# Convolutions accumulated in the projection's PSUM bank, scores moved into the transposes' bank, and a fourth bank for the SSD projections

## The chip, the core and the metric

One core of a Trainium2 chip runs the whole program. The metric is the device time of one execution in microseconds. TensorE (PE), VectorE (DVE), ScalarE (ACT) and GpSimd (POOL) compute, SyncE (SP) issues the loads and stores. Matmuls write to PSUM, which has eight banks of 128 partitions by 512 float32 values; VectorE and ScalarE read and write PSUM, GpSimd doesn't.

## What is computed

One step of a recurrent decoder layer for 2048 prompt tokens and 64 sample tokens (8 sequences of 8), with 1024 model dimensions. The tokens are normalised, projected with `w_in`, and go through three branches; the branches are gated, joined, projected with `w_out`, added to the input and normalised again. Cut to what matters here:

```python
proj = rmsnorm(x, norm_g) @ w_in
z, xbc, dt_raw, lru_x, lru_gate, s5_u, s5_gate = split(proj)
# SSD branch
xbc = silu(conv4(xbc, ssd_conv_w) + ssd_conv_b)        # depthwise, 4 taps
xs, bm, cm = split(xbc)
# per chunk of 128 tokens, per group of 4 heads:
scores = cm @ bm.T                                      # "scores"
y_diag = (scores * decay * dt) @ xs
y_off  = (cm @ h) * exp(acum);  h = chunk_decay * h + (bm * to_end * dt).T @ xs
y_ssd = rmsnorm((y_diag + y_off + d * xs) * silu(z))
# RG-LRU branch
xr = conv4(lru_x, lru_conv_w) + lru_conv_b
y_lru = linear_scan(f(xr @ lru_wa), g(xr @ lru_wx, xr)) * silu(lru_gate)
# S5 branch ...
out = x + concat(y_ssd, y_lru, y_s5) @ w_out
```

## The kernel before

The tokens stand in five segments: four of 512 prompt tokens (s = 0 to 3) and one of 64 sample tokens (s = 4). A projection (`in_proj`, L236 to L251) takes a block of 128 columns of `w_in` and one segment: 24 matmuls (eight parts of the contraction, each high by high, low by high and high by low in float16) add up in one PSUM bank, the tile `ps_mm`. The banks of the pool `pmm` (three of them) are taken in turn. The pool `ptp` has two banks (`ps_tp`, transposes), and the pool `pss` has three single ones with the tags "g", "y" and "s".

The program goes through these stages: the normalisation and the S5 branch, then the RG-LRU branch (`emit_lru`, about 430 to 705 us of the trace), then the SSD branch (`ssd_group` for four groups of heads, about 705 to 1380 us), then the output projection.

A channel block of the SSD branch (`channels` in `ssd_group`) runs so: ScalarE evicts the projection to `raw` in SBUF (`conv_raw`, L398), which ends the use of its bank. ScalarE writes the first tap and the bias to the tile `x` (L411), VectorE adds the other three taps in place (L413, three instructions), ScalarE takes the tanh of it into `th` (L699), and VectorE makes silu of the two (L700). The RG-LRU branch has the same convolution, without silu, into `xr`.

A chunk (`ssd_chunk`, 16 prompt chunks for each group) runs so: three transposes into `ps_tp` (L603, L604), of which VectorE makes `xdt` (L608) and ScalarE copies `bs` (L610); the scores matmul into the bank "g" (`ps_g`, L578), which ScalarE copies to `gm` (L587) and GpSimd masks (L588); VectorE multiplies the decays `e` with it (L589). Then come eight matmuls into the bank "y" (`ps_y`, L626 with `e`, L629 with the state `hst` and the decayed `ce`, which GpSimd makes at L596 out of a loaded row), the state product into the bank "s" (`ps_s`, L631), the state's update (L635 on GpSimd, L636 on VectorE) and the addition of `ps_y` to `x` (L640). The next chunk's `ps_y` waits for L640. The sample segment has one chunk for each group. The groups 2 and 3 also project their gates (`gated`, L710); those of the groups 0 and 1 were projected earlier and are loaded.

No order is written out by hand. A scheduler of the language orders each engine's instructions when the program is built, by a cost model of its own, within what dependences, tile buffers and banks allow; on the chip each engine then runs its list in order. Buffers that count here: `th` has two (the squares `sq` of the gated rows use them too), `ce` two, `raw` three, `x` five.

Of the kernel before, what the change touches and what calls it, by code (L numbers as in the profile page):

```python
# [43 lines left out]
def hymba_step_kernel(  # L44
# [16 lines left out]
    def bank(pool, tag, name):  # L61
        return pool.tile([128, 512], F32, name=name, tag=tag)
# [22 lines left out]
    def col(nm, i, src=cols):  # L85
        c = COL[nm] + i
        return src[:, c:c + 1]
# [145 lines left out]

    XH, XL = {}, {}

    def in_proj(w, s):  # L236

        n = SEGS[s][1]
        blocks = list(WB.values())
        for i, b in enumerate(blocks):  # L240
            if b.done is None and blocks[i - 6].left:
                b.age += 1
                if b.age > AGE:
                    b.finish()
            b.left = b.left or (b.w is w and s == 3)
        ps = bank(pmm, "mm", "ps_mm")
        for k in range(KD):
            P.matmul(ps[:, :n], lhsT=w[:, 0, k, :], rhs=XH[s][:, k, :], start=(k == 0), stop=False)  # L248
            P.matmul(ps[:, :n], lhsT=w[:, 0, k, :], rhs=XL[s][:, k, :], start=False, stop=False)  # L249
            P.matmul(ps[:, :n], lhsT=w[:, 1, k, :], rhs=XH[s][:, k, :], start=False, stop=(k == KD - 1))  # L250
        return ps[:, :n]  # L251
# [148 lines left out]
        G.tensor_copy(tl.halo, raw[:, SG:SG + 3])  # L400
        return raw

    def conv(out, raw, s, w, b):
        if s == 4:
            o = out.rearrange("p (b e) -> p b e", e=8)
            rv = raw.rearrange("p (b e) -> p b e", e=11)
            tap = [rv[:, :, j:j + 8] for j in range(4)]
        else:
            o = out
            tap = [raw[:, j:j + SG] for j in range(4)]  # L410
        A.activation(out=o, in_=tap[0], func=AF.Identity, scale=w[0], bias=b)  # L411
        for j in range(1, 4):
            V.scalar_tensor_tensor(o, tap[j], w[j], o, op0=ALU.mult, op1=ALU.add)  # L413

    def gate(ps, un2, s):

        n = SEGS[s][1]
        th = seg_tile("th", "th", s, st)
        pz = seg_tile("pz", "pz", s, st)
        A.activation(out=th, in_=ps, func=AF.Tanh, scale=un2)  # L420
        V.scalar_tensor_tensor(pz, th, 1.0, ps, op0=ALU.add, op1=ALU.mult)  # L421
        return pz
# [149 lines left out]

    sqacc = {}

    def scores(sp, g, BT, CT, q0, n, bcq, c):

        gp = bank(pss, "g", "ps_g")
        P.matmul(gp[:n, :n], lhsT=BT[:, q0:q0 + n], rhs=CT[:, q0:q0 + n], start=True, stop=True)  # L578
        e = sp.tile([128, 4, 128], F32, name="e", tag="e")
        gm = sp.tile([128, 128], F32, name="gm", tag="gm")[:n, :n]  # L580
        for h in range(4):
            A.activation(out=e[:n, h, :n], in_=bcq[:n, h, :n], func=AF.Relu, scale=-1.0, bias=acum[:n, c, 4 * g + h:4 * g + h + 1])  # L582
        A.activation(out=e[:n, :, :n], in_=e[:n, :, :n], func=AF.Exp, scale=-1.0)
        if c == 16:
            V.tensor_tensor(gm, gp[:n, :n], tri_s, op=ALU.mult)
        else:
            A.copy(gm, gp[:n, :n])  # L587
            G.affine_select(out=gm, in_=gm, pattern=[[1, n]], compare_op=ALU.is_ge, fill=0.0, base=0, channel_multiplier=-1)  # L588
        V.tensor_tensor(e[:n, :, :n], e[:n, :, :n], gm.unsqueeze(1).to_broadcast([n, 4, n]), op=ALU.mult)  # L589
        return e  # L590
# [8 lines left out]
    def transposed(sp, xs, BT, q0, n, g, c):  # L599

        tp = bank(ptp, "tp", "ps_tp")
        for j in range(2):
            P.transpose(tp[:n, j * 128:(j + 1) * 128], xs[j][:, q0:q0 + n], id32)  # L603
        P.transpose(tp[:n, 256:384], BT[:, q0:q0 + n], id32)  # L604
        xdt = sp.tile([128, 4, 64], F32, name="xdt", tag="xdt")
        xw = sp.tile([128, 4, 64], F32, name="xw", tag="xw")
        bs = sp.tile([128, 128], F32, name="bs", tag="bs")
        V.tensor_tensor(xdt[:n], tp[:n, 0:256].rearrange("p (h e) -> p h e", h=4),  # L608
                        dt_all[:n, c, 4 * g:4 * g + 4].unsqueeze(2).to_broadcast([n, 4, 64]), op=ALU.mult)
        A.copy(bs[:n], tp[:n, 256:384])  # L610
        G.tensor_tensor(xw[:n], xdt[:n], te[:n, c, 4 * g:4 * g + 4].unsqueeze(2).to_broadcast([n, 4, 64]), op=ALU.mult)
        return xdt, xw, bs

    def ssd_chunk(sp, g, xs, BT, CT, c, H):
        q0 = (c * 128) % SG
        bcq = sp.tile([128, 4, 128], F32, name="bcq", tag="bcq")
        S.dma_start(out=bcq, in_=aT[c, 4 * g:4 * g + 4, :].unsqueeze(0).to_broadcast([128, 4, 128]))
        xdt, xw, bs = transposed(sp, xs, BT, q0, 128, g, c)
        m = scores(sp, g, BT, CT, q0, 128, bcq, c)
        yp = bank(pss, "y", "ps_y")  # L620
        if c:
            ce = c_decayed(sp, CT, q0, 128, eT[c, 4 * g:4 * g + 4, :])
        o = [yp[64 * (h % 2):64 * (h % 2) + 64, (h // 2) * 128:(h // 2) * 128 + 128] for h in range(4)]
        for j in range(2):
            for h in (2 * j, 2 * j + 1):
                P.matmul(o[h], lhsT=xdt[:, h, :], rhs=m[:, h, :], start=True, stop=(c == 0))  # L626
            if c:
                for h in (2 * j, 2 * j + 1):
                    P.matmul(o[h], lhsT=H[:, h, :], rhs=ce[:, h, :], start=False, stop=True)  # L629
        ps = bank(pss, "s", "ps_s")  # L630
        P.matmul(ps[:, 0:256], lhsT=bs, rhs=xw.rearrange("p h e -> p (h e)"), start=True, stop=True)  # L631
        hn = sp.tile([128, 4, 64], F32, name="hst", tag="hst")
        spv = ps[:, 0:256].rearrange("p (h e) -> p h e", h=4)
        if c:
            G.tensor_tensor(hn, H, dec[:, c, 4 * g:4 * g + 4].unsqueeze(2).to_broadcast([128, 4, 64]), op=ALU.mult)  # L635
            V.tensor_tensor(hn, hn, spv, op=ALU.add)  # L636
        else:
            V.tensor_copy(hn, spv)
        for j in range(2):
            V.scalar_tensor_tensor(xs[j][:, q0:q0 + 128], xs[j][:, q0:q0 + 128], dpair[:, 2 * g + j:2 * g + j + 1],  # L640
                                   yp[:, j * 128:(j + 1) * 128], op0=ALU.mult, op1=ALU.add)
        return hn

    def ssd_sample(sp, g, xs, BT, CT):
# [4 lines left out]
        for q in range(2):  # L649
            hb = sp.tile([128, 4, 4, 64], F32, name="hb", tag="hb", bufs=2)  # L650
            S.dma_start(out=hb, in_=ssd_st[g, :, 4 * q:4 * q + 4])
            hbs.append(hb)
        xdt, xw, bs = transposed(sp, xs, BT, 0, n, g, 16)
        m = scores(sp, g, BT, CT, 0, n, bcq, 16)
        ce = c_decayed(sp, CT, 0, n, eTs[4 * g:4 * g + 4, :])
        for j in range(2):
            yp = bank(pss, "y", "ps_y")
# [9 lines left out]
        for q in range(2):  # L667
# [11 lines left out]
                V.tensor_tensor(hv, hv, ps, op=ALU.add)  # L679
            S.dma_start(out=o_ssd_s[g, :, 4 * q:4 * q + 4], in_=hb)  # L680

    def ssd_group(sx, sp, g, done):
        blks = [2 * g, 2 * g + 1, 8 + g, 12 + g]
        ws = [WB[c0] for c0 in SB(g)]
# [4 lines left out]
        def channels(i, s):  # L689

            w, un, _ = ws[i]
            b = blks[i]
            raw = conv_raw(in_proj(w, s), un, s, tls[i], stS[:, b, :])
            if s == 3:
                w_ahead()
            x = seg_tile("xxbc"[i] + str(i % 2), "x", s, sx if i < 2 else sp, SG, 5 if i < 2 else 2)
            conv(x, raw, s, [col("sconv_w", 16 * j + b, hcols) for j in range(4)], col("sconv_b", b, hcols))
            th = seg_tile("th", "th", s, st)
            A.activation(out=th, in_=x, func=AF.Tanh)  # L699
            V.scalar_tensor_tensor(x, th, 1.0, x, op0=ALU.add, op1=ALU.mult)  # L700
            return x

        def gated(j, s, y):
            k = 2 * g + j
            s0, n = SEGS[s]
            if k < ZE:
                pz = seg_tile("pz", "pz", s, st)
                S.dma_start(out=pz, in_=zb[k, :, s0:s0 + n])
            else:
                pz = gate(in_proj(WB[k][0], s), WB[k][2], s)  # L710
                if s == 3:
                    w_ahead()
            V.tensor_tensor(y, y, pz, op=ALU.mult)
            if g == 0 and j == 0:
                sqacc[s] = sx.tile([128, SEGS[s][1]], F32, name="sqacc", tag=f"sqacc{s}", bufs=1)
                rows[j].add(s, y, sqacc[s])
            else:
                sq = seg_tile("th", "sq", s, st)
                rows[j].add(s, y, sq)
                G.tensor_tensor(sqacc[s], sqacc[s], sq, op=ALU.add)  # L720
# [42 lines left out]
    def emit_lru(lp, blocks):  # L763
        for b in blocks:
# [8 lines left out]
            for grp in LRU_ORD:  # L773
                L = []
                for s in grp:
# [3 lines left out]
                        w_ahead()  # L779
                    raw = conv_raw(ps, wx[1], s, tail, stL[:, b, :])  # L780
                    xr = seg_tile("xr", "xr", s, lp, bufs=2)
                    conv(xr, raw, s, [col("lconv_w", 4 * j + b) for j in range(4)], col("lconv_b", b))
                    tr = seg_tile("tr", "tr", s, lp, bufs=2)
                    ti = seg_tile("ti", "ti", s, lp, bufs=2)
                    for q, dst, bn in ((0, tr, "lru_ba"), (1, ti, "lru_bx")):
# [719 lines left out]
```

## Time and profile before

| what | value |
|---|---|
| median of 3 runs | 1740.16 us (1739.29 to 1746.83) |
| the profiled execution | 1735.94 us, span of the trace 1734.2 us |
| PE busy | 1583.1 us, 91% of the span |
| DVE busy | 1142.8 us, 66% |
| ACT busy | 861.4 us, 50% |
| POOL busy | 567.7 us, 33% |
| granted TensorE clock, mean | 0.961 |

Busy time is the time in which an engine had an instruction in work. "L413 x192" in a row means 192 instructions of line 413. PEclk is the mean granted clock of TensorE, as a share of its full speed. The three numbers behind "ns" of a line's own view are the shortest, the median and the longest instruction.

### The profile page before, as it was taken

How to read it: one execution, taken by the hardware profiler on the slowest of the kernel's cores; microseconds unless marked ns; L12 is line 12 of the kernel's file. 1: busy time of each engine (PE TensorE's matmuls, PEld its weight loads, DVE VectorE, ACT ScalarE, POOL GpSimd, SP SyncE). 2: the span in 40 equal slices, each digit the busy share in tenths (PEclk: the TensorE clock that was granted, in tenths of full speed). 3: DMA queues.
4: the chain of work that ended last, by engine and by line, in shares of the span. 5: the costliest groups of instructions: out<-in, count | busy, mean ns of one | idle time of the engine just before them, and what ended most of it. 6: DMA issues, size and time to landing. Idle time of an engine off the chain costs nothing.

```text
span 1734.2 us, 26649 instructions
## 1 busy us (share of the span) xinstructions
PE 1583.1 (91%) x9465; PEld 815.7 (47%) x9465; DVE 1142.8 (66%) x2628; ACT 861.4 (50%) x1894; POOL 567.7 (33%) x837
## 2 busy tenths in 40 slices
PE   2689899889989999999999967999999699999998
PEld 1345444445444444455555544555554444444443
DVE  7991668899377766678868565677777744633332
ACT  4642434335498677657557444566766521422210
POOL 3542415775122111244545554544345200000000
PEclk8799999899999999999999987999999799999999
DMA  6761332223242542323334352243335441633100
GB/s 201 169 133 45 81 125 85 79 79 101 78 120 78 155 122 82 110 68 119 122 95 134 83 149 65 76 123 118 127 96 180 148 125 33 211 112 106 43 25 31
DMA packets 163077, 183.41 MB, mean 106 GB/s; under 512 B 85440, under 2 KB 111488, under 8 KB 162944
## 3 DMA queue, kind: packets, MB, share of 16 engines
q1 hardware_dynamic: 162944, 181.71, 35.5%
q8 instruction: 74, 1.21, 0.3%
q14 instruction: 59, 0.48, 0.1%
HBM read 127.09 MB, written 48.69 MB: 101 GB/s over the span
## 4 chain that ended last, share of the span: by engine, by line
PE 49%; DVE 6%; ACT 5%; issue 2%; DMA 2%; POOL 2%; SPq 0%; POOLq 0%; ACTq 0%; DVEq 0%
PE ps_mm L248 7%; PE ps_mm L249 7%; PE ps_mm L250 7%; PE ps_o L1233 6%; PE ps_o L1235 6%; PE ps_o L1234 6%; DVE x L413 2%; PE ps_y L626 2%; PE ps_s L631 2%; PE ps_y L629 1%; PE ps_g L578 1%; PE ps_tp L603 1%; DMA w<-in_w_blk_dram 1%; ACT e L582 1%; POOL ce L596 1%
## 5 line engine op out<-in xcount | busy, mean ns | idle before, releaser
L248 PE MATMUL ps_mm<-xh,whl 128*128 128x512 f16 x1280 | 493.4, 385 | 23.5 <-DVE pz L421 9.4
L249 PE MATMUL ps_mm<-xl,whl 128*128 128x512 f16 x1280 | 492.7, 385 | 0.0
L250 PE MATMUL ps_mm<-xh,whl 128*128 128x512 f16 x1280 | 491.5, 384 | 0.2 <-DVE whl L207 0.2
L249 PEld LDWEIGHTS <-whl 128*128 128x128 f16 x1600 | 156.1, 99 | 165.3 <-issue 34.9
L248 PEld LDWEIGHTS <-whl 128*128 128x128 f16 x1600 | 159.2, 101 | 155.6 <-issue 18.7
L250 PEld LDWEIGHTS <-whl 128*128 128x128 f16 x1600 | 156.4, 99 | 156.0 <-issue 18.1
L1233 PE MATMUL ps_o<-wo,yt 128*128 128x512 f16 x512 | 195.1, 381 | 10.1 <-ACT yt L1244 5.6
L1234 PE MATMUL ps_o<-wo,yt 128*128 128x512 f16 x512 | 195.1, 381 | 0.0
L1235 PE MATMUL ps_o<-wo,yt 128*128 128x512 f16 x512 | 194.2, 380 | 0.0
L413 DVE SCALAR_TENSOR_TENSOR x<-raw,hcols,x 128x512 f32<-128x512 f32 x192 | 160.7, 841 | 26.2 <-ACT x L411 23.5
L582 ACT ACTIVATE e<-bcq,acum 128x128 f32<-128x128 f32 (+1 forms) x272 | 86.1, 386 | 60.9 <-PE ps_y L626 54.2
L1244 ACT ACTIVATE yt<-y,rsc 128x256 f16<-128x256 f32 (+1 forms) x144 | 56.8, 477 | 106.9 <-PE ps_o L1235 81.1
L596 POOL TENSOR_TENSOR ce<-ce,x 128x512 f32<-128x512 f32 x60 | 83.7, 1405 | 73.3 <-DMA ce<-eT 36.6
L1408 ACT ACTIVATE yo<-res 128x1024 f32<-128x1024 f32 x16 | 16.8, 1050 | 152.0 <-DVE res L1253 152.0
L1253 DVE SCALAR_TENSOR_TENSOR res<-ps_o,rsu,res 128x512 f32<-128x512 f32 x32 | 24.0, 750 | 95.1 <-PE ps_o L1235 95.1
L421 DVE SCALAR_TENSOR_TENSOR pz<-th,ps_mm 128x512 f32<-128x512 f32 x64 | 43.7, 683 | 58.3 <-ACT th L420 57.7
L1233 PEld LDWEIGHTS <-yt 128*128 128x128 f16 x512 | 50.4, 98 | 66.4 <-ACT yt L1244 6.0
L1234 PEld LDWEIGHTS <-yt 128*128 128x128 f16 x512 | 50.3, 98 | 65.5 <-issue 5.9
L589 DVE TENSOR_TENSOR e<-e,gm 128x512 f32<-128x512 f32 (+1 forms) x68 | 56.2, 827 | 37.4 <-POOL gm L588 33.6
L1235 PEld LDWEIGHTS <-yt 128*128 128x128 f16 x512 | 50.2, 98 | 60.9 <-issue 0.6
L398 ACT ACTIVATE raw<-ps_mm,sc_out 128x512 f32<-128x512 f32 x80 | 54.2, 678 | 39.1 <-PE ps_mm L250 37.1
L420 ACT ACTIVATE th<-ps_mm,sc_out 128x512 f32<-128x512 f32 x64 | 43.6, 681 | 48.4 <-PE ps_mm L250 47.8
(455 smaller groups left out, 3063.6 us busy)
## 6 DMA issues: line engine op xcount, KB each, us to landing
w<-in_w_blk_dram SPq DMA_DIRECT2D x40, 512.0 KB
bcq<-aT SPq DMA_DIRECT2D x64, 256.0 KB
y<-ysp SPq DMA_DIRECT2D x16, 1024.0 KB
ce<-eT SPq DMA_DIRECT2D x60, 256.0 KB
xt<-in_x_dram SPq DMA_DIRECT2D x16, 512.0 KB
ysp<-x SPq DMA_DIRECT2D x32, 256.0 KB
wo<-in_w_out_dram SPq DMA_DIRECT2D x16, 512.0 KB
res<-in_x_dram SPq DMA_DIRECT2D x16, 512.0 KB
```

The lines of the kernel that those rows point to most:

```text
L248: P.matmul(ps[:, :n], lhsT=w[:, 0, k, :], rhs=XH[s][:, k, :], start=(k == 0), stop=False)
L249: P.matmul(ps[:, :n], lhsT=w[:, 0, k, :], rhs=XL[s][:, k, :], start=False, stop=False)
L250: P.matmul(ps[:, :n], lhsT=w[:, 1, k, :], rhs=XH[s][:, k, :], start=False, stop=(k == KD - 1))
L398: A.activation(out=raw[:, 3:SG + 3], in_=ps, func=AF.Copy, scale=un)
L413: V.scalar_tensor_tensor(o, tap[j], w[j], o, op0=ALU.mult, op1=ALU.add)
L582: A.activation(out=e[:n, h, :n], in_=bcq[:n, h, :n], func=AF.Relu, scale=-1.0, bias=acum[:n, c, 4 * g + h:4 * g + h + 1])
L589: V.tensor_tensor(e[:n, :, :n], e[:n, :, :n], gm.unsqueeze(1).to_broadcast([n, 4, n]), op=ALU.mult)
L596: G.tensor_tensor(ce[:, :, :n], ce[:, :, :n], CT[:, q0:q0 + n].unsqueeze(1).to_broadcast([128, 4, n]), op=ALU.mult)
L1233: P.matmul(ps, lhsT=h, rhs=w[:, 0, c], start=(k == 0), stop=False)
L1234: P.matmul(ps, lhsT=h, rhs=w[:, 1, c], start=False, stop=False)
L1235: P.matmul(ps, lhsT=l, rhs=w[:, 0, c], start=False, stop=(k == nk - 1))
L1244: A.activation(out=hl[:, k, 0, :n], in_=r[:, k, :n], func=AF.Copy, scale=c)
```

## The change

The convolution gets a second target, `acc`. ScalarE writes the first tap into the PSUM bank from which `raw` was just evicted, and VectorE adds the taps there. In the SSD branch all three taps stay in the bank, the tanh reads it, and the silu instruction, which reads it too, writes `x`. In the RG-LRU branch the third tap writes `xr`. The scores matmul writes the last 128 columns of the chunk's `ps_tp`, in place of the bank "g", and the SSD projections take their banks in turn from the three of `pmm` and from "g". The projections of the other stages keep their three banks.

```diff
-    def in_proj(w, s):
+    RING = []
+    def in_proj(w, s, ring=((pmm, "mm"),)):
+        RING.append(s)
...
-        ps = bank(pmm, "mm", "ps_mm")
+        ps = bank(*ring[len(RING) % len(ring)], "ps_mm")
...
-    def conv(out, raw, s, w, b):
+    def conv(out, acc, raw, s, w, b):
...
-            o = out
+            o = acc
             tap = [raw[:, j:j + SG] for j in range(4)]
         A.activation(out=o, in_=tap[0], func=AF.Identity, scale=w[0], bias=b)
         for j in range(1, 4):
-            V.scalar_tensor_tensor(o, tap[j], w[j], o, op0=ALU.mult, op1=ALU.add)
+            V.scalar_tensor_tensor(out if j == 3 else o, tap[j], w[j], o, op0=ALU.mult, op1=ALU.add)
...
-    def scores(sp, g, BT, CT, q0, n, bcq, c):
-        gp = bank(pss, "g", "ps_g")
+    def scores(sp, g, BT, CT, q0, n, bcq, c, tp):
+        gp = tp[:, 384:512]
...
+    MM4 = [(pmm, "mm")] * 3 + [(pss, "g")]
...
-            raw = conv_raw(in_proj(w, s), un, s, tls[i], stS[:, b, :])
+            ps = in_proj(w, s, MM4)
+            raw = conv_raw(ps, un, s, tls[i], stS[:, b, :])
...
-            conv(x, raw, s, [col("sconv_w", 16 * j + b, hcols) for j in range(4)], col("sconv_b", b, hcols))
+            conv(ps, ps, raw, s, [col("sconv_w", 16 * j + b, hcols) for j in range(4)], col("sconv_b", b, hcols))
             th = seg_tile("th", "th", s, st)
-            A.activation(out=th, in_=x, func=AF.Tanh)
-            V.scalar_tensor_tensor(x, th, 1.0, x, op0=ALU.add, op1=ALU.mult)
+            A.activation(out=th, in_=ps, func=AF.Tanh)
+            V.scalar_tensor_tensor(x, th, 1.0, ps, op0=ALU.add, op1=ALU.mult)
...
-                pz = gate(in_proj(WB[k][0], s), WB[k][2], s)
+                pz = gate(in_proj(WB[k][0], s, MM4), WB[k][2], s)
...
-                    conv(xr, raw, s, [col("lconv_w", 4 * j + b) for j in range(4)], col("lconv_b", b))
+                    conv(xr, ps, raw, s, [col("lconv_w", 4 * j + b) for j in range(4)], col("lconv_b", b))
```

The change gives the scheduler other dependences, so the order moves from the end of the S5 stage on. Three places follow; the lines of the changed kernel are shifted (L413 is L417 there, L578 is L582, L603 is L607, L626 is L630, L629 is L633, L631 is L635, L700 is L707).

First, VectorE at the first channel blocks of the SSD branch. Before:

```order
L413 SCALAR_TENSOR_TENSOR x_7399<-raw_7394,hcols_98,x_7399 128x512
L834 TENSOR_TENSOR lg_7349<-pz_7341,ti_7247 128x512
L413 SCALAR_TENSOR_TENSOR x_7399<-raw_7394,hcols_98,x_7399 128x512
L207 SCALAR_TENSOR_TENSOR whl_7347<-w32_7345,sc_out_7408,whl_7347 128x1024
L413 SCALAR_TENSOR_TENSOR x_7399<-raw_7394,hcols_98,x_7399 128x512
```

And in the changed kernel:

```order
L417 SCALAR_TENSOR_TENSOR ps_mm_7418<-raw_7443,hcols_98,ps_mm_7418 128x512
L458 TENSOR_SCALAR rsc_103<-rsc_103,sc_out_5409 128x1
L417 SCALAR_TENSOR_TENSOR ps_mm_7418<-raw_7443,hcols_98,ps_mm_7418 128x512
L707 SCALAR_TENSOR_TENSOR x_7448<-th_7453,ps_mm_7418 128x512
L417 SCALAR_TENSOR_TENSOR ps_mm_7456<-raw_7481,hcols_98,ps_mm_7456 128x512 x3
L707 SCALAR_TENSOR_TENSOR x_7486<-th_7491,ps_mm_7456 128x512
```

The taps read and write the projection's bank now, and `x` is written once, by the silu instruction.

Second, PE in the first segment of group 0, at the scores of the first two chunks, with the engine that each instruction waits for. Before:

```order
L578 MATMUL ps_g_7544<-x_7524,x_7486 128x128 [waits DVE_49]
L248 LDWEIGHTS whl_5824
L248 MATMUL ps_mm_7747<-xh_578,whl_5824 128x512
L249 LDWEIGHTS whl_5824
L249 MATMUL ps_mm_7747<-xl_579,whl_5824 128x512
L250 LDWEIGHTS whl_5824
L250 MATMUL ps_mm_7747<-xh_578,whl_5824 128x512
L603 MATMUL ps_tp_7612<-id32_81,x_7399 128x128 [waits Activation_49]
```

And in the changed kernel:

```order
L608 MATMUL ps_tp_7534<-id32_81,x_7486 128x128 [waits DVE_49]
L608 MATMUL ps_tp_7568<-id32_81,x_7486 128x128
...
L582 MATMUL ps_tp_7534<-x_7524,x_7486 128x128 [waits Activation_49]
L582 MATMUL ps_tp_7568<-x_7524,x_7486 128x128 [waits Activation_49]
...
L607 MATMUL ps_tp_7610<-id32_81,x_7399 128x128 [waits Activation_49]
```

The scores waited for VectorE's last operand `x` alone; now they stand behind ScalarE's `bs` copy out of the same bank, and the next chunks' transposes behind ScalarE's copy of the scores.

Third, PE at the end of group 1 (the last two prompt chunks of segment 3, then the first chunks of group 2). Before:

```order
L629 MATMUL ps_y_10614<-ce_10615,hst_10585 64x128 x2
L631 MATMUL ps_s_10626<-xw_10597,bs_10598 128x256
L626 MATMUL ps_y_10657<-e_10647,xdt_10639 64x128 x2
L629 MATMUL ps_y_10657<-ce_10658,hst_10628 64x128 x2
...
L631 MATMUL ps_s_10669<-xw_10640,bs_10641 128x256
L603 MATMUL ps_tp_10883<-id32_81,x_10748 128x128
L603 MATMUL ps_tp_10918<-id32_81,x_10748 128x128
L603 MATMUL ps_tp_10883<-id32_81,x_10797 128x128
L603 MATMUL ps_tp_10918<-id32_81,x_10797 128x128
L604 MATMUL ps_tp_10883<-id32_81,x_10835 128x128
L604 MATMUL ps_tp_10918<-id32_81,x_10835 128x128
L578 MATMUL ps_g_10893<-x_10873,x_10835 128x128
```

And in the changed kernel:

```order
L633 MATMUL ps_y_10581<-ce_10582,hst_10553 64x128 x2
L635 MATMUL ps_s_10593<-xw_10565,bs_10566 128x256
L635 MATMUL ps_s_10635<-xw_10607,bs_10608 128x256
L630 MATMUL ps_y_10623<-e_10613,xdt_10606 64x128 x2
L633 MATMUL ps_y_10623<-ce_10624,hst_10595 64x128 x2
...
L607 MATMUL ps_tp_10849<-id32_81,x_10714 128x128
L607 MATMUL ps_tp_10883<-id32_81,x_10714 128x128
L251 LDWEIGHTS whl_10411
L251 MATMUL ps_mm_11007<-xh_146,whl_10411 128x512
```

Before, all operands of group 2's first segment had been projected earlier, and its transposes and scores follow with no projection between; now projections of group 2 stand at that place.

## Rows read from the trace of the kernel before

**Rows 1.** The page's part 1: busy us, share of the span, instructions.

```profile
PE 1583.1 (91%) x9465; PEld 815.7 (47%) x9465; DVE 1142.8 (66%) x2628; ACT 861.4 (50%) x1894; POOL 567.7 (33%) x837
```

**Rows 2.** Stretches by stage: RG-LRU, then SSD. Second number: the stretch's length.

```profile
core 0: us, PE busy (x) PEld busy (x) DVE busy (x) ACT busy (x) POOL busy (x), PEclk, DMA share, GB/s
430.00:705.00 275.00, 256.25 (x1321) 122.84 (x1320) 177.64 (x374) 202.90 (x367) 47.60 (x84) 0.98 0.35 102
705.00:1380.00 675.00, 628.18 (x4258) 352.45 (x4257) 490.18 (x978) 396.35 (x922) 316.29 (x464) 0.95 0.38 114
```

**Rows 3.** Stretches of 20 us at the end of group 1 and of group 3.

```profile
1000.00:1020.00 20.00, 17.87 (x154) 11.27 (x153) 12.92 (x21) 10.91 (x30) 13.45 (x17) 0.91 0.42 116
1020.00:1040.00 20.00, 9.37 (x56) 5.36 (x54) 11.96 (x25) 8.12 (x22) 7.96 (x11) 0.70 0.65 181
1040.00:1060.00 20.00, 15.88 (x96) 9.81 (x96) 11.86 (x32) 9.24 (x28) 9.72 (x14) 0.79 0.24 59
1060.00:1080.00 20.00, 14.30 (x88) 7.34 (x86) 10.98 (x18) 10.87 (x26) 10.24 (x12) 0.74 0.32 92
1080.00:1100.00 20.00, 19.49 (x180) 12.41 (x179) 15.12 (x33) 12.75 (x36) 10.64 (x19) 1.00 0.37 99
...
1360.00:1380.00 20.00, 12.16 (x65) 9.91 (x64) 15.47 (x36) 10.68 (x21) 2.17 (x2) 0.50 0.48 152
```

**Rows 4.** PE's waits from 995 to 1085 us: us in total, times, longest.

```profile
PE ps_tp L603 <- DVE x L700: 8.1, 2, 5.9
PE ps_y L629 <- POOL ce L596: 6.5, 2, 4.4
...
PE ps_y L629 <- DVE hst L636: 2.1, 1, 2.1
PE ps_y L626 <- DVE e L589: 0.9, 1, 0.9
...
PE ps_y L626 <- DVE x L640: 0.3, 2, 0.2
```

**Rows 5.** PE's waits from 705 to 1380 us, one line.

```profile
PE ps_mm L248 <- ACT raw L398: 0.7, 1, 0.7
```

**Rows 6.** PE's waits from 430 to 705 us.

```profile
PE ps_mm L248 <- DVE pz L421: 5.8, 2, 3.1
```

**Rows 7.** Costliest groups, two lines: busy us, mean ns, idle before.

```profile
L413 DVE SCALAR_TENSOR_TENSOR x<-raw,hcols,x 128x512 f32<-128x512 f32 x192 | 160.7, 841 | 26.2 <-ACT x L411 23.5
...
L700 DVE SCALAR_TENSOR_TENSOR x<-th,x 128x512 f32<-128x512 f32 x64 | 54.5, 862 | 18.7 <-ACT th L699 17.3
...
L413 DVE SCALAR_TENSOR_TENSOR xr<-raw,cols,xr 128x512 f32<-128x512 f32 x48 | 38.1, 793 | 15.6 <-ACT xr L411 15.0
```

**Rows 8.** The lines' own views: ns shortest, median, longest; first and last start.

```profile
L413 DVE SCALAR_TENSOR_TENSOR x<-raw,hcols,x x192: 727/750/2071, 711.3 to 1338.7; 128x512 f32<-128x512 f32 x192
...
L700 DVE SCALAR_TENSOR_TENSOR x<-th,x x64: 675/690/2403, 715.8 to 1340.1; 128x512 f32<-128x512 f32 x64
...
L421 DVE SCALAR_TENSOR_TENSOR pz<-th,ps_mm x64: 655/686/690, 109.4 to 1379.2; 128x512 f32<-128x512 f32 x64
...
L1253 DVE SCALAR_TENSOR_TENSOR res<-ps_o,sc_out,res x32: 743/751/751, 1389.5 to 1705.5; 128x512 f32<-128x512 f32 x32
...
L398 ACT ACTIVATE raw<-ps_mm,sc_out x80: 662/674/704, 431.8 to 1335.4; 128x512 f32<-128x512 f32 x80
...
L411 ACT ACTIVATE x<-raw,hcols x64: 797/813/834, 709.3 to 1336.1; 128x512 f32<-128x512 f32 x64
...
L699 ACT ACTIVATE th<-x x64: 612/630/637, 715.1 to 1339.5; 128x512 f32<-128x512 f32 x64
```

**Rows 9.** Two readers of the transposes' bank, and who waited for L608.

```profile
L608 DVE TENSOR_TENSOR xdt<-ps_tp,dt_all x68: 405/418/426, 731.9 to 1352.6; 128x256 f32<-128x256 f32 x64, 64x256 f32<-64x256 f32 x4
...
  ACT bs L610: 14.8, 13
...
L610 ACT COPY bs<-ps_tp x68: 238/262/279, 732.3 to 1357.0; 128x128 f32<-128x128 f32 x64, 64x128 f32<-64x128 f32 x4
```

More of the change, by code (lines that the diff above doesn't have):

```diff
@@ L401, in conv_raw @@
         return raw
-    def conv(out, raw, s, w, b):
+    def conv(out, acc, raw, s, w, b):
         if s == 4:
-            o = out.rearrange("p (b e) -> p b e", e=8)
+            o, out = (x.rearrange("p (b e) -> p b e", e=8) for x in (acc, out))
             rv = raw.rearrange("p (b e) -> p b e", e=11)
@@ L611, in transposed @@
         G.tensor_tensor(xw[:n], xdt[:n], te[:n, c, 4 * g:4 * g + 4].unsqueeze(2).to_broadcast([n, 4, 64]), op=ALU.mult)
-        return xdt, xw, bs
+        return xdt, xw, bs, tp
     def ssd_chunk(sp, g, xs, BT, CT, c, H):
@@ L617, in ssd_chunk @@
         S.dma_start(out=bcq, in_=aT[c, 4 * g:4 * g + 4, :].unsqueeze(0).to_broadcast([128, 4, 128]))
-        xdt, xw, bs = transposed(sp, xs, BT, q0, 128, g, c)
-        m = scores(sp, g, BT, CT, q0, 128, bcq, c)
+        xdt, xw, bs, tp = transposed(sp, xs, BT, q0, 128, g, c)
+        m = scores(sp, g, BT, CT, q0, 128, bcq, c, tp)
         yp = bank(pss, "y", "ps_y")
@@ L652, in ssd_sample @@
             hbs.append(hb)
-        xdt, xw, bs = transposed(sp, xs, BT, 0, n, g, 16)
-        m = scores(sp, g, BT, CT, 0, n, bcq, 16)
+        xdt, xw, bs, tp = transposed(sp, xs, BT, 0, n, g, 16)
+        m = scores(sp, g, BT, CT, 0, n, bcq, 16, tp)
         ce = c_decayed(sp, CT, 0, n, eTs[4 * g:4 * g + 4, :])
```

## The prediction

> **What bounds the kernel now.** I read the page's busy shares first: PE works 91% of the span and VectorE 66% [rows 1], so time is lost only where PE waits or runs slowly. The stretches by stage show where. In the RG-LRU stage PE is idle for 275 - 256.25 = 18.8 us, in the SSD stage for 675 - 628.18 = 46.8 us, and VectorE is busy for 73% of the SSD stage [rows 2]. The change touches only these two stages (their order moves, and that of the last S5 steps). The fine stretches show that half of the SSD stage's idle time is one lump where group 1 ends and group 2 begins: from 1000 to 1080 us PE is idle for 2.13 + 10.63 + 4.12 + 5.70 = 22.6 us [rows 3]. The granted clock falls there too, to a mean of 0.91, 0.70, 0.79 and 0.74, time at both of TensorE's levels, 2.4 and 1.2 GHz; it fell after PE had begun to wait, and was full again from 1080 us. The waits there name the causes: transposes that waited for the silu of `x` (8.1 us), products that waited for `ce` (6.5), for the state (2.1), for `e` (0.9) and for L640 (0.3) [rows 4]. What the reader should see is that these are latencies of a chain of small steps on four engines. They show because PE had nothing else to run: in the order of before, all six steps from one chunk's product to the next in group 1's last and group 2's first segment have at most one projection matmul between them. A like end of group 3 (a mean clock of 0.50 [rows 3]) stays, because nothing is left to project there.
>
> **The change, part by part, against the profiled 1735.94 us.**
>
> *Order, the lump (A).* The order moves because a projection's bank is now held until the silu is done. Projections of group 2 can no longer run far ahead while its silu waits for buffers, and so they are left for the place where PE had nothing. The order shows it at the end of group 1. The lump's price is its idle 22.6 us, and what the slow clock cost in its busy time: 0.09 x 17.87 + 0.30 x 9.37 + 0.21 x 15.88 + 0.26 x 14.30 = 1.6 + 2.8 + 3.3 + 3.7 = 11.4 us [rows 3]. Together 34.0 us go. I take all of it; the waits that remain are priced next.
>
> *Order, short runs (B).* I counted, in the order of each kernel, the steps from one prompt chunk's product to the next in the same group with at most three 512-column projection matmuls between. Before there are 11: the six of the lump, two single ones, and three at the end of group 3. After there are 19: 7 in group 0, 7 in group 1, one in group 2, and one plus the three at the end in group 3. So there are 16 - 2 = 14 more short steps outside the lump and the end, one to three at a time, with projections on both sides. The lump's six steps waited 6.5 + 2.1 + 0.9 + 0.3 = 9.8 us, 1.6 each, and 0.9 without the longest wait (4.4 us, a late `ce` load) [rows 4]. I take the middle, 1.3, because a single step can meet a late load too, but rarely. 14 x 1.3 = 18.2 us come back. The bounds are what PE waited where only L640 was late, 0.3 / 2 = 0.15 us, and 1.6 us with a sixth of the lump's clock loss, 1.9, on top, 3.5: 2.1 and 49 us.
>
> *The scores' bank.* A chunk's scores used to need nothing but `x`; now they stand behind `xdt` and `bs`, the two reads of their bank. Those take 0.42 and 0.26 us, and `bs` already waits for `xdt`, though the two read different columns (13 times, 14.8 us) [rows 9]. That lengthens a chunk's chain by 0.68 us. On PE, the matmuls queued behind the scores (projections, state products) wait too when ScalarE is late. With projections in between it is hidden; in a short run it shows, and on top of the higher price an item of B then costs 1.6 + 0.68 = 2.3 us. I keep 1.3, since the scores of two chunks now stand in two banks, where the single "g" bank was handed from chunk to chunk. The Trainium skill, PSUM — Partial Sum Buffer, section on bank collisions, says to guard PSUM by bank and quadrant and not by address, which speaks against this sharing; the trace agrees, since `bs` waits for `xdt`. By addresses alone B would stay at 18.2 us, by the rule it can go to 32 us; that is the second rival.
>
> *The convolution's instructions (C).* In the SSD stage 192 steps of L413 take 841 ns on average but 750 in the median, with a longest of 2071; the same step takes 793 in the RG-LRU stage, where GpSimd is less busy (47.60 of 275 us against 316.29 of 675) [rows 2, 7, 8]. The long ones read two SBUF tensors while GpSimd works. With one input in PSUM this tail is absent: L421 ranges from 655 to 690 ns, L1253 from 743 to 751 [rows 8]. I take L1253's 751 for a tap, which has its form but for the target (bounds 686 and 841; a write to PSUM is in no row), and L421's 686 for the silu: 192 x 0.090 + 64 x 0.176 + 48 x 0.042 = 17 + 11 + 2 = 30 us less on VectorE. That work lies beside PE's in all but the runs of B, so I credit 2 us of the end (0 to 6). L411 and L699 change target and source; from 813 and 630 ns they can move by some 0.1 us either way, which ScalarE's idle time takes (396 busy of 675 us [rows 2]). The Trainium skill, VectorE: DVE Perf Modes, section Rules for kernel authors, advises copying out of PSUM first where many operations follow, which speaks against this edit; the medians of L413 and L1253, 750 and 751 ns, show no such cost for a PSUM input. By the access figures of Perfetto Trace Analysis, section Optimizing Scalar/DVE Operations (about 60 ns on SBUF, 125 on PSUM), 304 instructions would cost an estimated 20 us of VectorE time, beside PE.
>
> *Held banks (D).* A bank was free 0.67 us after its projection; now it is held for L398, L411, three taps and in the SSD stage the tanh and the silu: 0.67 + 0.81 + 3 x 0.75 = 3.7 us in the RG-LRU stage, and with 0.63 + 0.69 5.1 us in the SSD stage [rows 8], plus waits in the two queues. Queued behind a late bank are all later matmuls. In the SSD stage four banks cover it: most projections in the new order find their bank's last one three projections back. In the RG-LRU stage there are still three, and one is lent for the scales of the weights, so at some nine places only one other projection lies between. The nearest row is the gates' bank, held for two instructions: 3.1 us at the longest, in two waits of 5.8 us in all [rows 6]. I take 4 us, bounds 0 and 9 x 3.1 = 28.
>
> *The sum.* -34.0 + 18.2 - 2 + 4 = -13.8 us: 1722.1 for an execution like the profiled one. The median of the runs stands 4.2 us above that one, so 1726.3 us.
>
> **The rivals.**
>
> 1. *Short runs cost nearly nothing.* At 0.15 us each, with C at 6 and D at 0: -34.0 + 2.1 - 6 = -37.9, so 1702.3 us. For it: one to three late chunks leave PE too little idle time to build up waits as the lump did. Against it: `ce` is loaded only when one of its two buffers is free. 12%.
> 2. *The shared bank takes it back.* An item of B costs 2.3 us: -34.0 + 32 - 2 + 4 = 0, so 1740 us, no change. For it: `bs` waited for `xdt` 13 times already. 28%.
> 3. *Slower: short runs cost as much as the lump's.* At 3.5 us, clock included: -34.0 + 49 - 2 + 4 = +17, so 1757 us. It is a chunk chain that is bound by its `ce` load and by scores that start late, in groups 0 and 1, where few projections are left to fill in. It decides from 2.3 us each on. For it: 4.4 us for one `ce` in the trace. Against it: five of the seven in each group are single steps. 18%.
> 4. *Slower: the RG-LRU banks.* All nine places wait 3.1 us: -13.8 - 4 + 28 = +10, 1750 us. Against it: PE waited for a raw eviction for 0.7 us in the whole SSD stage [rows 5], so banks were rarely what was late. 5%.
>
> **How the numbers follow.** The forecast, 1726.3 us, has 37%. A measurement of this kernel can tell about 0.5%, 8.7 us, from no change. Faster by more than that hold the forecast and rival 1, less a little for the forecast's near edge, 0.48; within it rival 2 and that edge, 0.29; slower rivals 3 and 4, 0.23. The range runs from rival 1 to rival 3, 1702 to 1757 us, since less would leave out more than 2 in 10.
>
> **What would show it.** A: from the end of group 1 to the start of group 2 no stretch of 20 us has PE busy for under 14 us, and the clock's mean there stays over 0.9. B: PE's waits in groups 0 and 1, before that place, rise by 10 to 20 us, at `ps_y` and at the scores. C: the taps read 750 ns with no tail over 800, and the SSD stage's VectorE time falls by about 28 us. D: waits of L248 on L413 or L421 in the RG-LRU stage sum to no more than 10 us. The forecast is wrong if the scores, or the matmuls behind them, wait for ScalarE by over 2 us each, or if the lump comes back elsewhere.

## The result

The changed kernel takes 1814.38 us (median of 4 runs, 1812.12 to 1822.6), the kernel before 1741.6 us beside it: a ratio of 1.042 (95% interval 1.038 to 1.046), some 73 us slower, where 14 us faster was forecast. The profiled execution has a span of 1810.4 us, 76.2 more than before.

The page's part 1 of the changed kernel (busy us, share of the span, instructions), to be read against [rows 1]:

```profile
PE 1602.6 (89%) x9465; PEld 826.6 (46%) x9465; DVE 1099.2 (61%) x2628; ACT 855.8 (47%) x1892; POOL 524.9 (29%) x837
```

VectorE lost 44 us of work and GpSimd 43, and the span still grew, so no engine became the limit by its work. In the changed kernel L401 evicts to `raw` (L398 before), L415 writes the first tap (L411), L417 adds the others (L413), L706 is the tanh (L699), L425 the silu of a gate (L421), L446 a square of the gated rows (L442), L727 its sum on GpSimd (L720), L593 the product of `e` (L589), L614 the copy `bs` (L610), L591 the copy `gm` (L587), L640 the state's update (L636) and L644 the addition of `ps_y` to `x` (L640). The stretches by stage (RG-LRU, then SSD; columns as in [rows 2]):

```profile
core 0: us, PE busy (x) PEld busy (x) DVE busy (x) ACT busy (x) POOL busy (x), PEclk, DMA share, GB/s
430.00:717.00 287.00, 259.14 (x1320) 123.84 (x1319) 176.62 (x374) 200.70 (x365) 37.95 (x82) 0.96 0.33 98
717.00:1456.00 739.00, 643.45 (x4260) 360.79 (x4259) 447.06 (x982) 394.17 (x925) 282.71 (x464) 0.92 0.36 104
```

The RG-LRU stage is 12 us longer and the SSD stage 64; the stages before and after are as long as they were. In the SSD stage PE is idle for 95.6 us instead of 46.8, and the same work keeps it busy for 15.3 us more, while the granted clock's mean fell from 0.95 to 0.92, time at both levels, 2.4 and 1.2 GHz. PE's waits of that stage (us in total, times, longest) show what it waited for. Before, the list held 8.3 us of transposes on L700 and 3.6 us of projections on L421. Now it holds:

```profile
PE ps_mm L251 <- DVE pz L425: 22.4, 6, 4.6
PE ps_tp L607 <- DVE x L707: 14.7, 4, 5.3
PE ps_y L630 <- DVE x L644: 12.9, 7, 3.1
PE ps_y L630 <- DVE e L593: 6.2, 5, 3.1
...
PE ps_mm L251 <- DVE x L707: 5.2, 1, 5.2
...
PE ps_mm L251 <- DVE xs L707: 4.3, 1, 4.3
PE ps_tp L608 <- DVE x L707: 4.3, 1, 4.3
```

Projections (L251) now wait for a bank, 8 times and 31.9 us, and transposes (L607, L608) for the silu of their own segment, 19.0 us: both wait for silus that come late. The timeline of ScalarE shows why at one segment, the last one of group 0 (start us, length, instruction, idle before it):

```profile
818.49 0.69 ACT L401 ACTIVATE raw<-ps_mm,sc_out 128x512 f32<-128x512 f32 x1
...
820.12 0.77 ACT L415 ACTIVATE ps_mm<-raw,hcols 128x512 f32<-128x512 f32 x1
...
824.11 0.69 ACT L401 ACTIVATE raw<-ps_mm,sc_out 128x512 f32<-128x512 f32 x1 [2.70 <-PE ps_mm L253]
...
832.86 0.68 ACT L401 ACTIVATE raw<-ps_mm,sc_out 128x512 f32<-128x512 f32 x1
...
839.69 0.69 ACT L401 ACTIVATE raw<-ps_mm,sc_out 128x512 f32<-128x512 f32 x1 [0.83 <-PE ps_mm L253]
...
847.48 0.72 ACT L446 ACTIVATE sqacc<-x,unz 128x512 f32<-128x512 f32 x1
...
848.20 0.70 ACT L446 ACTIVATE sq<-x,unz 128x512 f32<-128x512 f32 x1
...
848.90 0.57 ACT L706 ACTIVATE th<-ps_mm 128x512 f32<-128x512 f32 x1
...
850.38 1.08 ACT L706 ACTIVATE th<-ps_mm 128x512 f32<-128x512 f32 x2 [0.90 <-POOL sqacc L727]
```

Its four blocks are evicted at 818.5, 824.1, 832.9 and 839.7 us. From an eviction to the end of its taps it takes 5 to 10 us. But the tanh of the first comes at 848.9, 30.4 us after its eviction, right behind the squares (L446) of the *previous* segment's gated rows, and the next two wait for GpSimd to add up such a square (L727). The squares `sq` take their buffers from the same two `th` as the tanh, and in program order the previous segment's squares come first. All four banks stand full until then, and from 839.7 to 853.8 us PE runs no projection. Over the stage's 64 blocks of 512 tokens (each bank followed by its name in the program's order), the time from the start of L401 to the end of L707, which the following calls the hold, is 15.7 us in the median and 35.3 at the longest, where the prediction counted 5.1.

In the groups 2 and 3 a gate is part of it: six of the eight bank waits, 22.4 of the 31.9 us, ended with the silu of a gate (L425). A gate's tanh writes into `th` too. Of the 16 gates of 512 tokens in these groups, ten stood in their banks for over 20 us after their projection in the kernel before, and eight for over 18 us in the changed one. The gates' hold is therefore not new; what is new is that the banks beside it are held too.

Before, the tanh waited for the same squares, in the lump of [rows 3] (the same view of the kernel before):

```profile
1038.72 0.72 ACT L442 ACTIVATE sq<-x,unz 128x512 f32<-128x512 f32 x1 [1.38 <-DVE x L713]
...
1039.44 0.70 ACT L442 ACTIVATE sq<-x,unz 128x512 f32<-128x512 f32 x1
...
1040.91 0.63 ACT L699 ACTIVATE th<-x 128x512 f32<-128x512 f32 x1 [0.67 <-POOL sqacc L720]
1042.25 1.18 ACT L699 ACTIVATE th<-x 128x512 f32<-128x512 f32 x2 [0.71 <-POOL sqacc L720]
```

There it held no bank. The blocks waited in the SBUF buffers of `x`. The two rows give the instructions of L413 and of L699 in the stretch from the SSD stage's start to that lump (busy us and count behind the stretch's length):

```profile
705.00:1035.00 330.00, 111.53 (x141) 0.98 0.38 112
```

```profile
705.00:1035.00 330.00, 21.27 (x40) 0.98 0.38 112
```

Three taps make a block, so 141 taps are 47 blocks; 40 had had their tanh. Seven blocks stood finished but for the tanh and silu. In the changed kernel at most four can, one in each bank.

### The profile page after: what moved, and what is told of

The parts are those of the page before. It is cut to its first block, busy times and chain, and to the rows that moved or that the text cites. A ratio compares the mean times of both kernels' runs of the same rounds, so it can differ in the third digit from the quotient of the medians.

```text
span 1810.4 us, 26568 instructions
## 1 busy us (share of the span) xinstructions
PE 1602.6 (89%) x9465; PEld 826.6 (46%) x9465; DVE 1099.2 (61%) x2628; ACT 855.8 (47%) x1892; POOL 524.9 (29%) x837
## 4 chain that ended last, share of the span: by engine, by line
PE 50%; DVE 5%; ACT 3%; DMA 2%; issue 1%; POOL 1%; SPq 0%; POOLq 0%; DVEq 0%
PE ps_mm L251 8%; PE ps_mm L252 8%; PE ps_mm L253 8%; PE ps_o L1240 6%; PE ps_o L1242 6%; PE ps_o L1241 6%; DVE ps_mm L417 2%; DMA ce<-eT 1%; PE ps_y L630 1%; PE ps_s L635 1%; PE ps_tp L607 1%; PE ps_y L633 1%; ACT e L586 1%; POOL ce L600 1%; PE ps_s L680 1%
## 5 line engine op out<-in xcount | busy, mean ns | idle before, releaser
L251 PE MATMUL ps_mm<-xh,whl 128*128 128x512 f16 x1280 | 501.7, 392 | 41.4 <-DVE pz L425 18.4
L252 PE MATMUL ps_mm<-xl,whl 128*128 128x512 f16 x1280 | 500.5, 391 | 0.0
L253 PE MATMUL ps_mm<-xh,whl 128*128 128x512 f16 x1280 | 498.0, 389 | 0.2 <-DVE whl L207 0.2
L252 PEld LDWEIGHTS <-whl 128*128 128x128 f16 x1600 | 159.5, 101 | 199.2 <-issue 69.7
L251 PEld LDWEIGHTS <-whl 128*128 128x128 f16 x1600 | 162.0, 103 | 164.0 <-issue 29.8
L253 PEld LDWEIGHTS <-whl 128*128 128x128 f16 x1600 | 159.9, 101 | 159.1 <-issue 25.2
L417 DVE SCALAR_TENSOR_TENSOR ps_mm<-raw,hcols,ps_mm 128x512 f32<-128x512 f32 x192 | 144.0, 752 | 51.6 <-ACT ps_mm L415 49.0
L600 POOL TENSOR_TENSOR ce<-ce,x 128x512 f32<-128x512 f32 x60 | 76.5, 1284 | 66.9 <-DMA ce<-eT 38.8
L401 ACT ACTIVATE raw<-ps_mm,sc_out 128x512 f32<-128x512 f32 x80 | 54.4, 681 | 77.2 <-PE ps_mm L253 76.8
L425 DVE SCALAR_TENSOR_TENSOR pz<-th,ps_mm 128x512 f32<-128x512 f32 x64 | 43.7, 683 | 57.4 <-ACT th L424 57.0
L630 PE MATMUL ps_y<-e,xdt 128*64 128x128 f32 x512 | 55.2, 296 | 20.8 <-DVE x L644 12.9
L612 DVE TENSOR_TENSOR xdt<-ps_tp,dt_all 128x256 f32<-128x256 f32 (+1 forms) x68 | 27.2, 419 | 72.4 <-PE ps_tp L608 43.0
```

Source lines behind the costliest of these rows:

```text
L401: A.activation(out=raw[:, 3:SG + 3], in_=ps, func=AF.Copy, scale=un)
L417: V.scalar_tensor_tensor(out if j == 3 else o, tap[j], w[j], o, op0=ALU.mult, op1=ALU.add)
L600: G.tensor_tensor(ce[:, :, :n], ce[:, :, :n], CT[:, q0:q0 + n].unsqueeze(1).to_broadcast([128, 4, n]), op=ALU.mult)
```

## The experiments

**Theory H** (held banks): the loss is the bank's hold while the tanh waits for `th`. **Theory S**: the loss is the scores, which now stand behind `bs` in the transposes' bank. "Squares over `pz`" means that the square of the gated rows is written over the gate's own tile, `pz`, and no longer into a buffer `th`. Every kernel gets an order of its own from the scheduler, and that is part of every difference here. The medians and ratios to the kernel before, run beside each:

| kernel | us | ratio (95%) |
|---|---|---|
| the change | 1814.4 | 1.042 (1.038 to 1.046) |
| scores_bank: change, convolutions in SBUF | 1767.6 | 1.017 (1.014 to 1.020) |
| conv_only: change, own scores bank, three banks | 1825.4 | 1.051 (1.048 to 1.054) |
| after_sq: change, squares over `pz` | 1707.1 | 0.982 (0.978 to 0.985) |
| before_sq: before, squares over `pz` | 1701.7 | 0.980 (0.977 to 0.983) |
| after_x: change, third tap into `x` | 1779.7 | 1.023 (1.020 to 1.026) |
| lru_only: before, RG-LRU taps in PSUM | 1747.5 | 1.007 (1.005 to 1.008) |
| scores3: before, shared scores bank | 1759.1 | 1.014 (1.010 to 1.018) |
| after_sq_lru: after_sq, RG-LRU taps in SBUF | 1698.9 | 0.978 (0.974 to 0.981) |
| scores_bank_sq | 1717.4 | 0.987 (0.985 to 0.990) |
| scores3_sq | 1707.3 | 0.983 (0.981 to 0.985) |
| ssdconv_sq: before_sq, SSD taps in PSUM | 1696.6 | 0.977 (0.974 to 0.980) |
| ssdconvx_sq: ssdconv_sq, third tap into `x` | 1693.0 | 0.974 (0.972 to 0.976) |

### The two halves of the change

scores_bank, against the changed kernel (and the RG-LRU call likewise):

```diff
-            conv(ps, ps, raw, s, ...)
+            conv(x, x, raw, s, ...)
-            A.activation(out=th, in_=ps, func=AF.Tanh)
-            V.scalar_tensor_tensor(x, th, 1.0, ps, op0=ALU.add, op1=ALU.mult)
+            A.activation(out=th, in_=x, func=AF.Tanh)
+            V.scalar_tensor_tensor(x, th, 1.0, x, op0=ALU.add, op1=ALU.mult)
```

> The changed kernel with every convolution back in SBUF; the shared scores bank and the four-bank ring stay. Theory H (held banks: the tanh that ends a bank's use waits for a buffer th, which the square of the earlier segment's gated rows held; a bank is held 16.5 us on average, up to 35): with the bank free after L401 the loss goes, 1725 to 1750 us, near before. Theory S (the scores, now behind bs in the transposes' bank, delay the chunks): stays near the changed kernel, 1795 to 1820 us.

1767.6 us lies between the two ranges and in neither: the convolutions in PSUM cost 2.5%, the rest of the change 1.7%. That fits H for the larger part, and leaves something for S.

conv_only, against the changed kernel:

```diff
-        gp = tp[:, 384:512]
+        gp = bank(pss, "g", "ps_g")
...
-    MM4 = [(pmm, "mm")] * 3 + [(pss, "g")]
+    MM4 = [(pmm, "mm")]
```

> The changed kernel with the scores back in a bank of their own and a ring of three banks; the convolutions stay in PSUM. H: three banks instead of four are held as long, so projections run ahead even less: 1825 to 1870 us. S: near before, 1730 to 1760 us.

1825.4 us, as H said, at the edge of its range. With the scores as before the loss is greater still, by 0.9%: where the convolutions stay in PSUM, the fourth bank brought more than sharing the scores' bank cost.

### The wait for `th`

```diff
-                sq = seg_tile("th", "sq", s, st)
-                rows[j].add(s, y, sq)
-                G.tensor_tensor(sqacc[s], sqacc[s], sq, op=ALU.add)
+                rows[j].add(s, y, pz)
+                G.tensor_tensor(sqacc[s], sqacc[s], pz, op=ALU.add)
```

> The changed kernel, but the square of the gated rows is written over pz instead of into a buffer th, so no tanh waits for the earlier segment's gated rows. H: the time from L401 to the end of L707 falls from a median of 15.7 us to 5 to 8, PE's 4 to 5 us waits of projections on L707 and L425 go, and the time falls to 1700 to 1735 us. S: the chunks wait as before, 1795 us or more.

> The kernel before with the same edit. H: the banks were free after 0.67 us there, so only the idle lump at the end of group 1 (34 us with its clock) can go, since silus of group 2 no longer wait for squares: 1700 to 1725 us. If the lump had another cause (late ce loads): 1735 to 1745 us.

This edit alone, which touches no bank, takes the changed kernel to 1707.1 us. The hold of a bank falls to a median of 7.1 us. Of PE's waits for a bank in the SSD stage these are left:

```profile
PE ps_mm L251 <- DVE pz L425: 1.5, 1, 1.5
PE ps_mm L251 <- DVE x L707: 0.9, 1, 0.9
```

31.9 us of bank waits have become 2.4. On the kernel before, the same edit is worth 2.0%, and the lump is gone (one stretch of before_sq; PE's busy time is the third number):

```profile
1000.00:1100.00 100.00, 99.18 (x724) 56.39 (x724) 64.72 (x135) 52.63 (x139) 50.70 (x77) 1.00 0.30 86
```

So the lump, too, hung on the silus' wait for squares. On the kernel before the edit is worth 35 us, on the changed one 107. Without the wait the change costs nothing that can be told (0.982 to 0.980); with it 4.2%. S is refuted as the main cause, since after_sq keeps the shared bank.

But the edit removes the wait and shortens the hold at once, so it doesn't separate the two. after_x does: the tanh still waits for `th`, and the bank comes free after the taps.

```diff
-            conv(ps, ps, raw, s, ...)
-            A.activation(out=th, in_=ps, func=AF.Tanh)
-            V.scalar_tensor_tensor(x, th, 1.0, ps, op0=ALU.add, op1=ALU.mult)
+            conv(x, ps, raw, s, ...)
+            A.activation(out=th, in_=x, func=AF.Tanh)
+            V.scalar_tensor_tensor(x, th, 1.0, x, op0=ALU.add, op1=ALU.mult)
```

> The changed kernel, but the third SSD tap writes x and the tanh and the silu work on x, as in the RG-LRU branch; squares still use th. So the bank is free after the taps (4 to 7 us) though the tanh waits for th as long as before. Theory H (the loss is the bank's hold during that wait): about scores_bank plus the RG-LRU's 0.7%, 1765 to 1785 us. Rival (the tanh's wait itself in the changed order is the loss, with or without the bank): 1800 to 1820 us.

1779.7 us, in H's range. From the end of the taps to the tanh's start a block waits even longer here, 36.1 us in the median for 7.8 in the changed kernel, since blocks can queue up in SBUF again, and yet the kernel is faster. The rival, that the wait itself is the loss, is refuted. Scores_bank and the RG-LRU's share (lru_only, below) give 1.017 + 0.007 = 1.024, and after_x has 1.023: by that sum, the SSD taps in PSUM cost nothing that can be told by themselves. Holding the bank on through the tanh's wait costs 1.042 - 1.023 = 1.9%, 34 us.

### The other terms

lru_only, against the kernel before (with `conv` as changed):

```diff
-                    conv(xr, raw, s, ...)
+                    conv(xr, ps, raw, s, ...)
```

> The kernel before with the RG-LRU convolutions alone in PSUM. The changed kernel's RG-LRU stage took 287 us for 275. If that is the held banks of this branch, 1746 to 1754 us here (before: about 1737 to 1741). If it came from the other order that the SSD edits give: 1735 to 1743 us.

0.66% (0.48 to 0.84), some 11.5 us. PE's waits in its RG-LRU stage have two new lines. The first is mostly one wait of 5.5 us on a third tap, some 20 us into the stage:

```profile
PE ps_mm L251 <- DVE xr L417: 6.7, 3, 5.5
PE ps_lg L794 <- ACT tr L795: 4.3, 1, 4.3
```

scores3, against the kernel before:

```diff
-        gp = bank(pss, "g", "ps_g")
+        gp = tp[:, 384:512]
```

> The kernel before with the scores in the transposes' bank, and no other edit (three banks, convolutions in SBUF, the freed bank unused). It splits the 30 us that the shared bank and the four-bank ring cost together. If the shared bank costs it (its chain bs, gm and the next transposes in one bank): 1760 to 1775 us. If the fourth bank does, by letting projections run further ahead of the silus so that PE has none left where group 1 ends: 1735 to 1750 us.

1.4%, some 24 us and a little under the range for the shared bank. So it is mostly the shared bank, not the fourth one, that scores_bank paid for (1.014 of 1.017). PE's waits name little of it:

```profile
PE ps_tp L582 <- ACT bs L614: 5.6, 10, 1.3
...
PE ps_tp L607 <- ACT gm L591: 2.9, 4, 1.8
```

Scores behind `bs` and transposes behind `gm` are 8.5 us, against 1.2 + 1.4 us for `bs` and `gm` before. The rest came with another order and isn't separated. So the 4.2% are, as far as parts add up, 1.9 for the hold in the SSD stage, 0.7 for the RG-LRU taps and 1.7 for the shared and the fourth bank. Four kernels with the squares over `pz`, their other edits those shown above, try what is left of it when no silu waits:

> scores_bank (shared scores bank, four banks, convolutions in SBUF) with squares over pz. If the shared bank's 24 us were the longer chain of every chunk: before_sq (1702) plus 15 to 25, 1717 to 1727 us. If they showed only where chunk follows chunk without projections, which the edit removes: 1697 to 1707 us.

> scores3 (scores in the transposes' bank, three banks, convolutions in SBUF) with squares over pz. scores_bank_sq stood 0.7% over before_sq. If the shared bank's longer chain is that: 1.010 to 1.014 times less gain here too, ratio to before 0.985 to 0.990, 1712 to 1722 us. If the fourth bank's order is: ratio 0.978 to 0.983, 1700 to 1709 us.

> The changed kernel with squares over pz (after_sq, 1707 us) and the RG-LRU convolutions back in SBUF. If these convolutions cost some 10 us: 1694 to 1700 us, a little under before_sq (1702). If they cost nothing: 1704 to 1710 us.

> The kernel before with squares over pz (before_sq, 1702 us) and the SSD convolutions in PSUM, scores in their own bank, three banks. H says that a held bank costs only by its wait for th, which is gone: with a hold of 5 to 8 us three banks nearly do, 1695 to 1715 us. If holding a bank through the five steps costs by itself: 1725 us or more.

Over before_sq (0.980), the shared bank stands at 0.983 with three banks (the intervals overlap), at 0.987 with four: scores_bank_sq fell where the longer chain was expected and scores3_sq where the fourth bank was, so neither reading holds alone. Between ssdconv_sq and after_sq_lru, where the SSD convolutions are in PSUM, the shared and the fourth bank together make 0.1%, which can't be told from nothing. So most of the 24 us hung on the silus' wait or on the order around it; a cost of 0 to 0.7% is left open. The RG-LRU taps cost 0.4% here (after_sq to after_sq_lru), within the intervals.

> ssdconv_sq (SSD convolutions in PSUM, three banks, squares over pz, 1697 us) with the third tap written to x, so that a bank is held some 1.5 us less (through the taps, not the silu). If hold time still counts at 7 us: 1688 to 1694 us. If it doesn't: 1694 to 1700 us; the silu then reads two SBUF inputs again, with its long tail beside GpSimd.

ssdconvx_sq (before_sq, the SSD taps in PSUM with the third one into `x`) is the fastest kernel, 1693.0 us, 2.6% under the kernel before. It is 0.6% under before_sq, the intervals just apart; it can't be told from ssdconv_sq.

## Why the prediction was wrong

**Held banks (D), the step that failed.** It put the SSD hold at 5.1 us "plus waits in the two queues" and its cost at nothing, because "four banks cover it". The hold was 15.7 us in the median, three times that. Of its mean of 16.5 us, 5.5 go to the end of the taps, the queues included, 9.6 until the tanh begins, and 1.4 are tanh and silu: what ends it late is a buffer more than the queues. after_x prices the term at 34 us, and after_sq, with its order, at some 71 (107 less the 35 that the edit brings with the banks as before). The prediction read "transposes that waited for the silu of `x`" [rows 4] and stopped there. One step further back, at the tanh's own wait in the trace of before, stood `sqacc` L720, and behind that a queue of seven blocks. The nearest row that it took, 3.1 us for a gate's bank, is what PE waited in the RG-LRU stage, and not how long a bank is held: the gates of the groups 2 and 3 stood in theirs for up to 97 us. It said of step A that projections can no longer run ahead while the silu waits for buffers, and entered only the gain of that. In the RG-LRU stage, +4 was taken inside bounds of 0 to 28, and lru_only measured 11.5; the sign named for it, waits on L417 (L413 before) or L425 of no more than 10 us, held with 6.2, so that sign didn't show the cost.

**The lump (A).** Its price fits: before_sq removes it and gains 35 us, for 34.0. That the new order would remove it was only half so. In the changed kernel the products of group 1's last segment begin at 1036 us, and those of group 2's first end by 1100. The stretches there:

```profile
1020.00:1040.00 20.00, 20.00 (x107) 10.61 (x106) 15.27 (x30) 8.33 (x17) 8.08 (x14) 0.99 0.42 140
1040.00:1060.00 20.00, 13.99 (x91) 7.94 (x89) 11.66 (x30) 10.53 (x28) 7.80 (x14) 0.86 0.48 140
1060.00:1080.00 20.00, 18.42 (x91) 9.75 (x92) 7.37 (x19) 4.60 (x11) 6.62 (x9) 0.88 0.11 32
1080.00:1100.00 20.00, 17.25 (x115) 9.26 (x113) 10.53 (x22) 12.29 (x31) 5.93 (x14) 1.00 0.31 86
```

PE is idle for 0 + 6.01 + 1.58 + 2.75 = 10.3 us, for 22.6 [rows 3], and the clock's mean is at 0.99, 0.86, 0.88 and 1.00. The signs named for A (no stretch under 14 us, a mean over 0.9) were missed, by 0.01 us in one stretch and by 0.04 and 0.02 in two. Waits of 4 to 5 us like those now also stand at nearly every other segment's end.

**Short runs (B).** 18.2 us were forecast. PE's waits of chunk products and of the state in the groups 0 and 1, from 717 to 1055 us, are

```profile
PE ps_y L630 <- DVE x L644: 10.3, 5, 3.1
...
PE ps_y L630 <- DVE e L593: 3.0, 4, 1.1
PE ps_s L635 <- DVE hst L640: 2.1, 2, 1.1
PE ps_y L664 <- DVE e L593: 1.8, 2, 1.1
...
PE ps_y L630 <- DVE sc_m L116: 0.7, 2, 0.3
PE ps_y L664 <- DVE xs L670: 0.4, 1, 0.4
```

They sum to 18.3 us. Of these, 2.1 us fall into the last segment of group 1, where the lump was, and 2.2 are the sample chunks' (L664), which the forecast didn't count: 14 us are left. The kernel before has 0.7 us in its groups 0 and 1 up to 1000 us. The term was of the right order, and the line that it named, `ps_y`, is the right one. None of them waits for `ce`, though, from which a part of the price was taken: L644 is what is late, so the size is partly luck. In after_sq, with its other order, the waits on L644 are gone.

**The scores' bank.** It was taken as hidden but in the runs of B, where it could make some 14 us more (rival 2). Alone, on the kernel before, it cost 24 us. The Trainium skill, PSUM — Partial Sum Buffer, section on bank collisions, asks for a guard by bank rather than by address. The program keeps one, and the trace shows its price: scores waited for `bs`, which reads other columns of the bank, 10 times and 5.6 us in scores3.

**The instructions (C).** Right in kind. Each line's shortest, median and longest ns, and below it groups of the SSD stage (busy us, mean ns, idle before), against [rows 7, 8]:

```profile
L417 DVE SCALAR_TENSOR_TENSOR ps_mm<-raw,hcols,ps_mm x192: 731/753/758, 722.5 to 1415.0; 128x512 f32<-128x512 f32 x192
```

```profile
L707 DVE SCALAR_TENSOR_TENSOR x<-th,ps_mm x64: 672/686/690, 729.2 to 1417.0; 128x512 f32<-128x512 f32 x64
```

```profile
L593 DVE TENSOR_TENSOR e<-e,gm 128x512 f32<-128x512 f32 x64 | 46.1, 729 | 38.2 <-POOL gm L592 38.1
...
L417 DVE SCALAR_TENSOR_TENSOR ps_mm<-raws,hcols,ps_mm 128x64 f32<-128x64 f32 x48 | 13.7, 286 | 1.0 <-ACT ps_mm L415 0.4
```

The tail of L413 (2071 ns) and L700 (2403) is gone, and the medians are 753 and 686 ns, for 751 and 686 taken. VectorE's time in the stage fell by 43 us for a forecast 28. The 48 sample taps, which the sum left out, went from a mean of 474 to 286 ns (9 us), and `e` from 843 to 729 (8 us), though no operand of it moved; why isn't shown. The worth of C on the end was put at 2 us; ssdconv_sq and ssdconvx_sq gain 0.3 and 0.6% on before_sq, of which the first can't be told from nothing.

**The rivals.** All four left the SSD hold out. The slower ones (1757 and 1750 us) stopped short of 1814: they took what the SSD stage could lose from the short runs, and D had bounds for the RG-LRU stage alone.

## What to carry to other kernels

Before a value is left in PSUM through more steps, follow the last of those steps back to everything that it waits for, its output buffer too: here it was a buffer shared with a later use. A queue of finished blocks in SBUF is run-ahead that the profile doesn't list as such; count it (one line's instructions against the next line's), since in banks only so many fit. And where such a wait is behind a lump of idle time, mend the wait itself: squares written elsewhere were worth 35 us here, with no bank moved.

## What the runs showed of the hardware

A tap with its accumulator in PSUM, read and written, took 753 ns in the median, for 750 in SBUF [rows 8], and ScalarE's first tap from SBUF to PSUM 782 ns for 813. The Trainium skill, VectorE: DVE Perf Modes, section Rules for kernel authors, offers a copy out of PSUM first where many operations follow; for the instructions' time the medians show no need of it here. Coming out of the bank sooner was worth 34 us all the same, with the third tap into `x` (after_x) and no copy.

The long tail of the taps before goes with GpSimd: of the 192 taps of L413 into `x`, 35 took over 800 ns, and every one of them ran beside an instruction of GpSimd with two tensor inputs; of the 157 others 39 did. In the changed kernel, with one input in PSUM, the longest took 758 ns.

PE's idle time in the changed SSD stage is a dozen stretches of 4 to 5.3 us, one of 6.1 at its end, and short ones, where before it had four over 4 us, two in the lump and two at the end of group 3. The stage's mean clock was 0.92, for 0.95 before, and PE's busy time there rose by 15 of the 64 us lost.
